# A hybrid encoder step: cached keys transposed on VectorE instead of TensorE, their loads cut in quarters on ScalarE's queue, and the sample's attention output stored once per batch

## The chip, the cores and the metric

The kernel runs on one core of one Trainium2 chip. The metric is the device time of one execution, in microseconds (us). Before the change it is 2877.0 us, the median of three runs (2876.0 to 2877.55).

## The reference

One layer of a streaming encoder is computed for two request groups that share the weights: a prompt of 2048 tokens, and a sample group of 8 batches of 16 new tokens, each batch with 1024 cached tokens. Everything is float32, D_MODEL is 1024.

```python
h = rms_norm(x, norm_g)
(a_x,a_b,a_c,a_z, g_q,g_f,g_i,g_z, s_q,s_k,s_v,s_z, m_a,m_b,m_c) = split_cols(h @ w_in)
# A: gated convolution  B: HGRN2 recurrence  C: stick-breaking attention, 8 heads of 64
z = einsum('bqhd,bkhd->bhqk', q, k) / 8
log_1mb = where(causal, log_sigmoid(-z), 0)
rest = cumsum(log_1mb, reverse) - log_1mb
A = where(causal, exp(log_sigmoid(z) + rest), 0);  o_sb = A @ v
# sample group: k = concat(cache_k (8, 1024, 8, 64), new keys), v likewise
m = sigmoid(m_a)*(o_a@wb_a) + sigmoid(m_b)*(o_b@wb_b) + sigmoid(m_c)*(o_c@wb_c)
return x + m @ w_out, and the new caches and states
```

The change touches branch C of the sample group alone: the scores of its 16 queries against the 1024 cached keys, and where its output is kept.

## The kernel before

The 17 tiles of 128 tokens (tile 0 is the sample group) are projected in three groups. In each group a list of jobs runs over the columns of `w_in`. A job multiplies a slice of weights with the normalised, transposed tokens: `proj_chan` (the matmul at L710, 24 of them for one accumulator) or `proj_tok` (L721). There are two accumulators in PSUM, which ScalarE or VectorE empty. To keep float32 accuracy every product is three passes over a high and a low part. The split weights of the first group are stored in DRAM (`W`) and loaded again by the later groups, 1 MB at a time (L208) or in two halves (L201); three weight buffers stand ready.

Other work is written as Python generators that the matmul loops advance: each `yield` returns a cost, and a background queue runs as far as its credit allows. So the place of a step in the program is set by these costs. `hbg` holds the recurrence of branch B (matmul L1039 between VectorE steps L1028 to L1040), `bg` the attention; in the second group `bg` holds `sample_attention()`, which this change is about. A planner of the tile framework then fixes the order on each engine from what it expects to be ready, so that an instruction can run ahead of others that the code has earlier. At run time every engine and every DMA queue works through its own order, and an instruction that waits holds back all behind it.

`sample_attention()` walks over 8 batches with three segments each (24 in all), of 3, 3 and 2 blocks of 128 cached tokens, so 64 blocks. For a segment:

- `keys(m)` brings the keys into the form that the scores need, head dimension on the partitions. Per block, SyncE issues one load of 256 KB (L455; 128 tokens by 512 columns, 2 KB per row) into `kc` (three buffers, shared with a few loads at either end), TensorE transposes it in four 128 by 128 pieces into PSUM (L458), and ScalarE copies the bank into `kt` (L459; two buffers of one segment each). The generator then yields a cost of 1.3.
- `scores` multiplies queries and keys (L476) and applies the two sigmoids on ScalarE (L483, L485), the scan and the product on VectorE (L489, L490).
- `turned` transposes the weights of a segment (L499) and loads the values (L506); `values` multiplies them (L522).

After the last segment of a batch the accumulator holds 128 rows (8 heads by 16 tokens) by 128 columns, of which each row needs one half of 64. ScalarE copies it to `od`, and eight stores of SyncE (L529), one per head, put the 16 by 64 pieces in their place in `OCS` (128 tokens by 512). At the end one load (L548) brings `OCS` back, and four transposes and a gate finish the branch.

## Time and profile before

| | |
|---|---|
| median of the runs | 2877.0 us |
| the profiled execution | 2876.11 us, its span 2873.2 us |
| TensorE (matmul) busy | 2853.0 us, 99% of the span |
| VectorE, ScalarE, GpSimd busy | 1546.5 us (54%), 1018.7 us (35%), 331.8 us (12%) |
| granted TensorE clock | 1.00 |
| moved by DMA | 649.76 MB in 370475 packets, mean 226 GB/s |
| first and last transpose of cached keys (L458) | 599.1 and 1138.5 us |

The page gives for each engine the time in which it had an instruction under way, and then follows the work that ended last back through what released each step. A wait counts only where it is on that chain. The DMA share is the mean busy share of the core's 16 DMA engines; it can read a little over 1, since packets overlap in an engine. A packet is one contiguous piece; 33481 of the packets are under 512 bytes, nearly all of them the reports of a DMA's end, up to 16 for each DMA.

### The profile page before, as it was taken

The page shows a single profiled execution, that of the slowest core. Times are in us where ns is not written, and L with a number is a line of the kernel's source. Part 1 is how long each engine was busy: PE and PEld are TensorE (multiplying, and loading weights), DVE is VectorE, ACT ScalarE, POOL GpSimd, SP SyncE. Part 2 cuts the span into 40 slices and gives each one's busy share as a digit, 9 for nine tenths or more (in the row PEclk, how much of TensorE's full clock was granted, in tenths as well). Part 3 has the DMA queues.
Part 4 walks back from the last instruction along what each step waited for, and adds up shares of the span by engine and source line. Part 5 has one row for each costly group of instructions (what it writes and reads, how often), then busy time and mean ns, then how long its engine had stood idle before and what let it go on. Part 6 is the DMA issues. An engine that isn't in the chain of part 4 may idle for free.

```text
span 2873.2 us, 51723 instructions
## 1 busy us (share of the span) xinstructions
PE 2853.0 (99%) x19479; PEld 2662.3 (93%) x19479; DVE 1546.5 (54%) x3304; ACT 1018.7 (35%) x2375; POOL 331.8 (12%) x802
## 2 busy tenths in 40 slices
PE   9999999999999999999999999999999999999999
PEld 9999999999999999999999999999998888787888
DVE  5454635641344442545434747557485876867743
ACT  4333222242233332213334444434444444544420
POOL 3110000111200000001323111111010011010100
PEclk9999999999999999999999999999999999999999
DMA  8887777777678887746766454544447877878876
GB/s 306 305 276 247 231 241 244 231 243 243 212 249 266 276 265 243 243 167 192 237 215 202 146 173 136 173 139 151 144 145 238 286 234 239 266 250 266 271 250 210
DMA packets 370475, 649.76 MB, mean 226 GB/s; under 512 B 33481, under 2 KB 246306, under 8 KB 339506
## 3 DMA queue, kind: packets, MB, share of 16 engines
q1 hardware_dynamic: 369458, 644.36, 68.2%
q8 instruction: 154, 2.52, 0.4%
q0 software_dynamic: 768, 2.10, 0.2%
q14 instruction: 95, 0.78, 0.1%
HBM read 447.06 MB, written 199.27 MB: 225 GB/s over the span
## 4 chain that ended last, share of the span: by engine, by line
PE 76%; DVE 2%; DMA 2%; issue 1%; ACT 0%; POOL 0%; SPq 0%; DVEq 0%; POOLq 0%; ACTq 0%
PE acc L710 33%; PE acc L721 10%; PE acc L1440 9%; PE acc L1471 6%; PE pv L359 4%; PE tp L310 4%; PE z L330 2%; PE z L329 2%; PE z L1039 1%; PE tp L458 1%; DMA gate<-GM 1%; PE pv L522 1%; PE z L476 0%; PE hg L1086 0%; PE hg L826 0%
## 5 line engine op out<-in xcount | busy, mean ns | idle before, releaser
L710 PE MATMUL acc<-hx,w 128*128 128x384 f32 (+1 forms) x6816 | 1251.8, 333 | 0.1
L710 PEld LDWEIGHTS acc<-hx,w 128*128 128x128 f32 x6816 | 1106.5, 188 | 21.9 <-issue 15.2
L721 PE MATMUL acc<-w,hx 128*128 128x256 f32 x2544 | 328.6, 284 | 1.8 <-DVE hx L176 0.9
L342 DVE TENSOR_TENSOR_SCAN pr<-snb,carry 128x513 f32<-128x513 f32 x192 | 246.5, 1284 | 153.3 <-ACT snb L333 151.7
L721 PEld LDWEIGHTS acc<-w,hx 128*128 128x128 f32 x2544 | 310.9, 188 | 5.0 <-DVE hx L176 1.7
L311 ACT COPY aT<-tp 128x512 f32<-128x512 f32 (+2 forms) x320 | 167.6, 524 | 375.2 <-PE tp L310 361.3
L710 PE MATMUL acc<-hx,wst 128*128 128x384 f32 x1248 | 247.2, 344 | 0.0
L1440 PE MATMUL acc<-o,w 128*128 128x512 f32 (+2 forms) x1080 | 234.7, 363 | 1.8 <-DMA o<-OX 1.8
L333 ACT ACTIVATE snb<-z 128x512 f32<-128x512 f32 (+2 forms) x320 | 172.4, 539 | 144.5 <-PE z L330 140.4
L710 PEld LDWEIGHTS acc<-hx,wst 128*128 128x128 f32 x1248 | 215.4, 188 | 6.4 <-issue 3.7
L1440 PEld LDWEIGHTS acc<-o,w 128*128 128x128 f32 x1080 | 185.1, 188 | 33.8 <-issue 5.3
L347 DVE TENSOR_TENSOR sp<-sp,pr 128x512 f32<-128x512 f32 (+2 forms) x320 | 195.3, 611 | 29.2 <-POOL sp L338 3.7
L342 DVE TENSOR_TENSOR_SCAN pr<-snb,one 128x129 f32<-128x129 f32 (+3 forms) x128 | 114.4, 894 | 123.9 <-POOL snb L338 123.6
L310 PE MATMUL tp<-idf,sp 128*128 128x128 f32 x1088 | 171.3, 273 | 2.5 <-ACT aT L311 1.5
L335 ACT ACTIVATE sp<-z 128x512 f32<-128x512 f32 (+2 forms) x320 | 171.5, 536 | 0.0
L1471 PE MATMUL acc<-w,mh 128*128 128x256 f32 x816 | 161.2, 285 | 1.0 <-DVE yt L1479 0.8
L1176 ACT ACTIVATE gm<-acc 128x384 f32<-128x384 f32 (+1 forms) x144 | 68.2, 474 | 230.4 <-PE acc L710 197.5
L310 PEld LDWEIGHTS tp<-idf,sp 128*128 128x128 f32 x1088 | 131.8, 141 | 19.3 <-issue 4.4
L176 DVE TENSOR_TENSOR w<-wst,w 128x1024 fp32r<-128x1024 f32 x72 | 88.1, 1223 | 110.7 <-ACT w L175 107.9
L1471 PEld LDWEIGHTS acc<-w,mh 128*128 128x128 f32 x816 | 131.0, 188 | 7.2 <-issue 4.2
L329 PE MATMUL z<-Kt,Q 128*128 128x512 f32 (+2 forms) x320 | 128.8, 403 | 0.3 <-ACT sp L335 0.2
L359 PE MATMUL pv<-aT,Vt 128*64 128x512 f32 (+3 forms) x640 | 128.1, 535 | 0.0
(299 smaller groups left out, 3570.1 us busy)
## 6 DMA issues: line engine op xcount, KB each, us to landing
w<-W SPq DMA_DIRECT2D x168, 1024.0 KB, 6.0
W<-w SPq DMA_DIRECT2D x72, 1024.0 KB, 5.0
wst<-W SPq DMA_DIRECT2D x112, 512.0 KB, 5.1
wst<-in_w_in_dram SPq DMA_DIRECT2D x72, 512.0 KB, 5.1
GM<-gm SPq DMA_DIRECT2D x120, 192.0 KB, 3.7
W<-mwp SPq DMA_DIRECT2D x40, 512.0 KB, 4.2
Kt<-KT SPq DMA_DIRECT2D x160, 128.0 KB, 3.1
o<-OX SPq DMA_DIRECT2D x72, 256.0 KB, 4.7
```

Source lines behind the costliest of these rows:

```text
L310: nc.tensor.transpose(tp[:, j * P:(j + 1) * P], sp[:, j * P:(j + 1) * P], idf)
L311: nc.scalar.copy(aT[:, e, 0:nb, i * P:(i + 1) * P], tp[:, :w].rearrange("p (b q) -> p b q", q=P))
L329: nc.tensor.matmul(z[:, :w], Q1[:, i * P:(i + 1) * P], Kt[:, :w], start=True, stop=False)
L333: nc.scalar.activation(sn[:, 512 - w:512], z[:, :w], AF.Sigmoid, scale=-0.125)
L335: nc.scalar.activation(sp[:, :w], z[:, :w], AF.Sigmoid, scale=0.125)
L342: nc.vector.tensor_tensor_scan(pr[:, 512 - w:513][:, ::-1], s_in, s_in, one if diag else carry[e][i], ALU.mult, ALU.bypass)
L347: nc.vector.tensor_tensor(sp[:, :w], sp[:, :w], pr[:, 513 - w:513], ALU.mult)
L359: nc.tensor.matmul(pv[64 * e:64 * e + 64, c0:n], Vt[:, j, e], aT[:, e, j, c0:n], start=first and j == 0, stop=last and j == nb - 1, skip_g ...
L710: nc.tensor.matmul(acc[:, :n], w[0][a][:, k], hT[b][:, k, :n], start=k == 0 and i == 0, stop=k == KB - 1 and i == 2)
L721: nc.tensor.matmul(acc[:, :256], hT[b][:, k, ti * P:(ti + 1) * P], w[k // 4][a][:, k % 4], start=k == 0 and i == 0, stop=k == KB - 1 and i ...
L1440: nc.tensor.matmul(acc[:, :n], w[0][a][:, k, dd * P:(dd + 1) * P], box[x][b][:, k, sl], start=k == 0 and i == 0, stop=k == 3 and i == 2)
L1471: nc.tensor.matmul(acc[:, :256], box["l" if b else "h"][:, k, ti * P:(ti + 1) * P], w[k // 4][a][:, k % 4], start=k == 0 and i == 0, stop= ...
```

## The change

1. `kc` becomes four-dimensional (128 partitions; 4 pairs of heads, 4 groups of 32 tokens, 32 columns), the same 256 KB. The one load on SyncE's queue becomes four loads on ScalarE's queue, one per quarter of 32 partitions. Quarter `a` fetches, for each of the 128 tokens and each pair of heads, the 32 columns of that quarter: contiguous pieces of 128 bytes.
2. The four TensorE transposes and ScalarE's copy out of PSUM become one VectorE transpose that turns every 32 by 32 block of `kc` and writes `kt`. What the 128 by 128 transpose did across blocks, the address pattern of the loads does.
3. `OCS` keeps the whole `od` of a batch (128 by 128) in one store instead of eight; at the end eight loads, one per head, pick the halves instead of one load.

The costs of the yields stay as they are.

```diff
-    OCS = dram.tile([P, 512], F32, name="OCS")
+    OCS = dram.tile([NB, P, 2, 64], F32, name="OCS")
...
             for bi in range(blocks(m)):
                 blk = 3 * sg + bi
-                kc = sa.tile([P, 512], F32, tag="cst", name="kc", bufs=3)
-                nc.sync.dma_start(kc, cache_k[0, b, blk * P:(blk + 1) * P].rearrange("t h d -> t (h d)"))
-                tp = ps_tp()
-                for h in range(4):
-                    nc.tensor.transpose(tp[:, h * P:(h + 1) * P], kc[:, h * P:(h + 1) * P], idf)
-                nc.scalar.copy(kt[:, :, bi * P:(bi + 1) * P], tp.rearrange("p (h t) -> p h t", h=4))
+                kc = sa.tile([P, 4, 4, 32], F32, tag="cst", name="kc", bufs=3)
+                keys_ = cache_k[0, b, blk * P:(blk + 1) * P].rearrange("(c p) h d -> p c (h d)", p=32)
+                keys_ = keys_.rearrange("p c (h x) -> p h c x", x=P)
+                for a in range(4):
+                    nc.scalar.dma_start(kc[32 * a:32 * a + 32], keys_[:, :, :, 32 * a:32 * a + 32])
+                nc.vector.transpose(kt[:, :, bi * P:(bi + 1) * P].rearrange("p h (c q) -> p h c q", q=32), kc)
                 yield 1.3
...
                 nc.scalar.copy(od, pv[:, 0:P])
-                for h in range(8):
-                    nc.sync.dma_start(OCS[b * TS:(b + 1) * TS, h * 64:(h + 1) * 64],
-                                      od[h * TS:(h + 1) * TS, 64 * (h % 2):64 * (h % 2) + 64])
+                nc.sync.dma_start(OCS[b].rearrange("r e d -> r (e d)"), od)
...
         oc = sa.tile([P, 512], F32, tag="cst", name="oc", bufs=3)
-        nc.sync.dma_start(oc, OCS)
+        for h in range(8):
+            nc.sync.dma_start(oc[:, h * 64:(h + 1) * 64], OCS[:, h * TS:(h + 1) * TS, h % 2])
```

## Rows read from the trace of the kernel before

**Rows 1.** The page: busy time by engine; shares of the last chain by line.

```profile
PE 2853.0 (99%) x19479; PEld 2662.3 (93%) x19479; DVE 1546.5 (54%) x3304; ACT 1018.7 (35%) x2375; POOL 331.8 (12%) x802
...
PE acc L710 33%; PE acc L721 10%; PE acc L1440 9%; PE acc L1471 6%; PE pv L359 4%; PE tp L310 4%; PE z L330 2%; PE z L329 2%; PE z L1039 1%; PE tp L458 1%; DMA gate<-GM 1%; PE pv L522 1%; PE z L476 0%; PE hg L1086 0%; PE hg L826 0%
```

**Rows 2.** Chain of waits, 560 to 1150 us: by line; one piece (start, us).

```profile
by line: PE acc L710 56.0%; PE acc L721 23.2%; PE tp L458 4.8%; PE pv L522 3.1%; PE z L476 2.4%; PE z L1039 2.1%; PE tp L499 1.3%; PE hg L826 0.9%; DMA xt<-in_x_prompt_dram 0.7%; PE hg L1086 0.5%; PE tp L1088 0.5%; PE hg L1084 0.5%; PE z L1
...
818.53 4.42 PE acc L710 x24
```

**Rows 3.** Stretches: start:end, length, busy us of each engine, granted clock, DMA share, GB/s.

```profile
560.00:1150.00 590.00, 587.23 (x4588) 566.38 (x4587) 226.15 (x587) 187.50 (x469) 52.38 (x92) 1.00 0.76 250
...
560.00:580.00 20.00, 19.39 (x130) 18.77 (x128) 10.64 (x35) 4.76 (x11) 3.96 (x4) 1.00 0.86 298
...
1060.00:1080.00 20.00, 20.00 (x147) 18.45 (x140) 2.87 (x4) 6.74 (x14) 0.00 (x0) 1.00 0.91 306
...
1120.00:1140.00 20.00, 20.00 (x147) 19.05 (x147) 8.41 (x23) 6.70 (x18) 0.00 (x0) 1.00 0.82 283
```

**Rows 4.** The timeline from 842 to 867 us: start, us, engine, line, operation.

```profile
842.78 0.42 DVE L1046 TENSOR_TENSOR Kd<-hgk,X 128x256 f32<-128x256 f32 x1
...
843.12 0.30 DVE L1040 COPY_PREDICATED sc<-lmask,z 128x128 f32<-128x128 int32 x1
...
845.03 0.47 PEld L458 LDWEIGHTS tp<-idf,kc 128*128 128x128 f32 x4
...
845.47 1.00 PEld L710 LDWEIGHTS acc<-hx,w 128*128 128x128 f32 x6
...
845.77 0.33 SPq L455 DMA_DIRECT2D kc<-in_cache_k_dram  x1
...
858.20 3.84 SPq L529 DMA_DIRECT2D OCS<-od  x8
...
866.98 0.47 PEld L458 LDWEIGHTS tp<-idf,kc 128*128 128x128 f32 x4
```

**Rows 5.** DMA packets from 560 to 1150 us: count, MB, sizes.

```profile
DMA packets 78082, 147.57 MB, mean 250 GB/s; under 512 B 8834, under 2 KB 43906, under 8 KB 72374
```

**Rows 6.** DMA from 205 to 206 us; queue: packets, MB, share of 16 engines.

```profile
DMA packets 603, 0.31 MB, mean 308 GB/s; under 512 B 1, under 2 KB 603, under 8 KB 603
...
q1 hardware_dynamic: 603, 0.31, 104.6%
```

**Rows 7.** DMA from 22.4 to 22.7 us, the same two rows.

```profile
DMA packets 213, 0.09 MB, mean 309 GB/s; under 512 B 146, under 2 KB 213, under 8 KB 213
...
q1 hardware_dynamic: 213, 0.09, 110.4%
```

**Rows 8.** DMA from 697.8 to 699 us, the same two rows.

```profile
DMA packets 96, 0.01 MB, mean 10 GB/s; under 512 B 96, under 2 KB 96, under 8 KB 96
...
q1 hardware_dynamic: 96, 0.01, 7.8%
```

**Rows 9.** DMA from 698.4 to 698.6 us, the same two rows.

```profile
DMA packets 4, 0.00 MB, mean 1 GB/s; under 512 B 4, under 2 KB 4, under 8 KB 4
...
q1 hardware_dynamic: 4, 0.00, 1.5%
```

**Rows 10.** Groups by line, whole span: count | busy us, mean ns | idle.

```profile
L459 ACT COPY kt<-tp 128x512 f32<-128x512 f32 x64 | 37.5, 588 | 58.6 <-PE tp L458 58.3
...
L347 DVE TENSOR_TENSOR sp<-sp,pr 128x512 f32<-128x512 f32 (+2 forms) x320 | 195.3, 611 | 29.2 <-POOL sp L338 3.7 <-DVE pr L342 0.5
```

**Rows 11.** Issue durations of the key loads on SyncE: ns min/median/max.

```profile
L455 SPq DMA_DIRECT2D kc<-in_cache_k_dram x64: 327/383/1494, 563.2 to 1119.0; - x64
```

**Rows 12.** Waits: who for whom, us in total, times, longest.

```profile
SPq L455 <- PE tp L458: 52.9, 24, 7.5
...
ACT w L175 <- DMA wst<-in_w_in_dram: 17.4, 10, 3.2
...
PE acc L1440 <- DMA o<-OX: 1.8, 1, 1.8
```

## The prediction

> **What bounds the kernel now.** I read the page first. TensorE is busy for 99% of the span, and the chain that ended last runs through its lines; the cached keys' transposes (L458) hold 1% of it [rows 1]. The change lives in one stage, so I then took the chain of waits, the table of stretches and the DMA view from 560 to 1150 us, which holds the keys' loads and transposes. There TensorE is busy 587.23 of 590 us at a granted clock of 1.00 (the level of 2.4 GHz), L458 holds 4.8% of the chain, VectorE is busy 226.15 us, ScalarE 187.50 us, and the 16 DMA engines have a mean share of 0.76 [rows 2, 3]. So two resources matter: TensorE, which sets the end, and DMA, which has a quarter to spare.
>
> **TensorE loses the transposes.** 4.8% of 590 us is 28.3 us. The timeline gives the same: weight loads of one block's transposes start at 845.03 and the next matmul's at 845.47, 0.44 us, times 64 blocks 28.2 us [rows 2, 4]. L458's whole busy time counts overlap with its neighbours twice, and I don't use it. Term: -28.3 us; no cover hides it, because TensorE has the next matmul at hand, but something else may take its place.
>
> **DMA gets small packets.** 64 blocks times 4 loads times 512 pieces (32 tokens, 4 groups, 4 pairs) are 131072 packets of 128 bytes. They replace 64 x 128 = 8192 packets of 2 KB. What goes: 0.76 x 16 x 590 us moved 147.57 MB, so 20.6 GB/s for an engine, 99.6 ns for 2 KB, and 8192 x 99.6 / 16 = 51 us of all engines [rows 3, 5]. What comes has no row, so I bound it. From 205 to 206 us there are only packets of 512 bytes: 1.046 x 16 x 1000 ns / 603 = 27.8 ns [rows 6]. From 22.4 to 22.7 us 146 packets are smaller (the gains' broadcast loads of 256 bytes) and 67 have 512: 1.104 x 4800 ns = 5299, less 67 x 27.8, leaves 23.5 ns each, on a full DMA [rows 7]. From 697.8 to 699 us the only traffic is the old OCS store, 256-byte pieces and as many end reports: 1498 ns / 96 = 15.6 ns on average [rows 8]; four reports alone take 1.5% of 3200 ns, 12 ns each [rows 9], which leaves 19.2 for 256 bytes on an idle DMA. 128 bytes therefore lie between 12 ns (a report) and 27.8 ns (a packet of 512). Carrying each pair half-way on gives 15.6 ns idle (between 12 and 19.2) and 21.4 ns full (as far below 23.5 as half of the step from 27.8). The stage is between the two; I take 18.5 ns, so 131072 x 18.5 / 16 = 152 us, plus 192 further loads' reports (2 us): net +103 us of all engines. At the ends: +49 us and +179 us.
>
> The stage had 0.76 x 590 = 448 us of DMA work; it would have 551 us in 590 - 28 = 562 us, 98% on average. That is not even: the 29 stretches of 20 us between 560 and 1140 lie between 0.51 and 0.91, 0.86 in the first and 0.82 in the last, mean 0.77 [rows 3]. Spreading the 103 us evenly (3.5 us to each) and setting each stretch against 19.04 us, 16 of the 29 overflow by 18.8 us together; if a full DMA reads 1.05, as it does with 512-byte packets [rows 6], 9 overflow by 6.4 us. The loads are a segment ahead, not more (the load issued at 845.77, right behind the transposes that free its buffer, is for the block transposed at 866.98 [rows 4], three blocks on), so little is smoothed between stretches. Term: +12.6 us, the middle; ends 0 (12 ns) and 49 to 74 us (27.8 ns), for which I take 62.
>
> The Trainium skill ("DMA: Bandwidth & Descriptors", Specifications) states that transfers below 512 bytes are slower, as the DMA engine reads, modifies and writes there. By that rule 128 bytes cost no less than 512 do. The trace agrees only in part: 256-byte pieces took 19.2 to 23.5 ns against 27.8. The rule's result is the second rival.
>
> **ScalarE gets issues, loses copies.** The 64 copies go, 37.5 us [rows 10]. 256 issues come. No load is issued on ScalarE before; on SyncE the issue of a key load takes 0.383 us, at least 0.327 [rows 11], and eight OCS stores in a row take 3.84 us, 0.48 each [rows 4]. So 84 to 123 us, and ScalarE goes from 187.5 to 234 to 273 us of 562: it is no bound, but its queue stands still in lumps. A block's four issues hold it for up to 1.9 us, a segment's twelve for 5.8 us if they come together, and behind them wait the copies and sigmoids that empty accumulators. An accumulator takes 4.42 us to fill [rows 2], and there are two, so one lump of four is covered, and twelve in a row delay the next by up to 5.8 + 0.5 - 4.4 = 1.9 us. Over 24 segments that is 0 to 46 us. I take 5, near the lower end, because loads wait for buffers that free one at a time as VectorE finishes.
>
> **VectorE gets 64 transposes.** There is no such row. A pass over 128x512 in float32 with two inputs takes 0.611 us [rows 10]; four predicated copies of 128x128 would be 1.2 us [rows 4]. So 39 to 77 us; I take 39, the same shape. VectorE then has 265 us of 562 and is no bound. The new wait is the transpose's, for four loads: behind it stand the recurrence's steps, for whose results TensorE waits (L1039). Whether it bites depends on the order. The planner does move instructions: L1046 starts at 842.78, before L1040 at 843.12, which the code has first [rows 4]. Where ScalarE waits for loads placed in this manner, 10 of 72 were late, 17.4 us together, at most 3.2 [rows 12]: 0.24 us for each, which for 64 blocks is 15 us at most and 0 if loads are a segment ahead. It is in the 5 us above.
>
> **SyncE and the sample's output.** SyncE loses 64 issues and stands 52.9 us less behind key buffers [rows 12], and 64 stores become 8 (8 x 0.48 us less 0.48, for each batch); at the end seven loads come, 3.4 us, after seven stores fewer. Only weight and activation loads gain, and TensorE waited for those 1.8 us in the whole run [rows 12]: 0, and at most 1.8 us won.
>
> **Sum.** -28.3 + 12.6 + 5 = -10.7 us. The profiled execution took 2876.1 us, its span 2873.2, and the median is 0.9 above it. From the median: 2866 us. Its own range runs from the full relief, 2848, to where a measurement can't tell it from no change (0.2%, 5.8 us), 2871.
>
> **Rivals.** (1) TensorE's time goes wholly to DMA and queue waits: the two plus terms come to 22 to 34 us instead of 17.6, which the 18.8 us of overflow and 5 to 10 for the queues already make. For it: an average of 98% with 16 full stretches. Against: a full DMA reads 1.05. 2877 us.
>
> (2) Small packets cost as much as 512 bytes do, by packet and not by bytes. DMA then has 627 us of work in a stage of 562 us, and keys come late in nearly every stretch: -28.3 + 62 = +34, 2911 us, up to +70 if the DMA only fills to 95%. For it: halving the packet from 512 to 256 saved only 4.3 of 27.8 ns. Against: an idle DMA took 19.2. It decides the sign from about 20 ns on if nothing is smoothed.
>
> (3) ScalarE's queue: twelve issues stand together in each segment, or wait for a key buffer, while an accumulator waits to be emptied. 24 x 1.9 = 46 us: -28.3 + 12.6 + 46 = +30, 2907 us. It turns the sign once a segment costs TensorE (28.3 - 12.6) / 24 = 0.65 us. For it: nothing on that queue was ever issued before, and the order there was free of such lumps. Against: ScalarE is idle for two thirds of the stage.
>
> That the transposes stay on TensorE's path in another form can't be: L458 is gone.
>
> **How the numbers follow.** The forecast has 0.45, rival (1) 0.19, (2) 0.19, (3) 0.17. That makes faster by over 0.2% 0.45, within 0.2% 0.19, slower 0.36. The range runs from 2848 (all relief, no cost) to 2925, past the centres of both slower rivals; above it stay their tails.
>
> **What would show it.** Right: L458 and L459 gone, the stretch from 599 to 1139 us shorter by 10 to 28 us, a DMA share there above 0.9, some 204000 packets there in place of 78082, TensorE without long idle times. Packet price: a share over 1 with idle TensorE behind keys would show rival (2). TensorE waiting for ScalarE's copies, with DMA issues ahead of them on its queue, shows rival (3). VectorE idle behind the loads of `kc`, with TensorE waiting for L1034 to L1040, would make my placing of the wait wrong. A VectorE transpose well above 1.2 us would make its term wrong.

## The result and the profile after

The changed kernel took 2886.93 us (median of 12 runs), the kernel before 2874.90 us in the 12 runs beside them: ratio 1.0040, 95% interval [1.0029, 1.0051]. It is slower by 12.0 us where I had forecast faster by 10.7 us. The range held the time, but only because it was drawn past the slower rivals; the sign was wrong. The profiled execution took 2884.56 us, its span is 2882.7 us.

The page of the changed kernel: busy time by engine and shares of the last chain by line (old L710, L721 and L1440 are now L711, L722 and L1441).

```profile
PE 2838.9 (98%) x19223; PEld 2643.8 (92%) x19223; DVE 1583.8 (55%) x3368; ACT 984.0 (34%) x2311; POOL 331.2 (11%) x802
...
PE acc L711 27%; PE acc L1441 10%; PE acc L722 8%; PE acc L1472 7%; PE pv L360 4%; PE tp L311 4%; DMA kc<-in_cache_k_dram 3%; PE z L331 2%; PE z L330 2%; PE z L1040 1%; DMA vc<-in_cache_v_dram 1%; DMA xt<-in_x_prompt_dram 1%; PE pv L524 0%;
```

Against [rows 1] the transposes' line is gone from the chain and TensorE is busy 14 us less, but the span is 9.5 us longer, and the keys' transfers (`kc`) hold 3% of the chain, which [rows 1] does not have. The next view is the table of stretches, with the columns of [rows 3].

```profile
560.00:1150.00 590.00, 563.86 (x4274) 539.46 (x4273) 260.52 (x643) 151.95 (x402) 50.30 (x88) 0.99 0.88 248
...
960.00:980.00 20.00, 20.00 (x156) 19.65 (x155) 12.36 (x41) 4.48 (x13) 0.00 (x0) 1.00 1.10 284
...
1060.00:1080.00 20.00, 19.69 (x127) 18.33 (x123) 4.18 (x6) 4.25 (x9) 0.00 (x0) 0.95 0.84 222
...
1140.00:1160.00 20.00, 17.29 (x112) 15.68 (x111) 12.21 (x39) 4.25 (x10) 0.21 (x1) 0.83 0.63 185
```

TensorE is busy 563.86 of 590 us, where before it was busy 587.23 [rows 3]; 26 us of it are idle now. The granted clock, 1.00 in every stretch before, is 0.95 and 0.83 in two that hold pauses of TensorE. Its levels are 1.2 and 2.4 GHz, so 0.83 is what a third of the stretch at the lower one gives. DMA's mean share went from 0.76 to 0.88 while the rate fell from 250 to 248 GB/s [rows 3]; five of the 31 stretches of 20 us from 560 to 1180 read 1.01 to 1.10, the last of them at 960. The packets of this stage, as in [rows 5], and the two queues that carry most:

```profile
DMA packets 202403, 146.38 MB, mean 248 GB/s; under 512 B 141232, under 2 KB 176813, under 8 KB 196717
...
q1 hardware_dynamic: 66893, 128.08, 67.7%
q10 hardware_dynamic: 135168, 16.79, 19.5%
```

The new queue, q10, is ScalarE's. Its 135168 packets are the 131072 pieces of 128 bytes and 4096 reports, in 19.5% of 16 x 590 us: 13.6 ns for a packet.

The chain of waits from 560 to 1180 us, by line, beside [rows 2]; below it, who waited for whom in this stretch (us in total, times, longest).

```profile
by line: PE acc L711 32.3%; PE acc L722 15.8%; DMA kc<-in_cache_k_dram 15.4%; DMA vc<-in_cache_v_dram 2.9%; PE pv L524 2.3%; DMA mwx<-in_w_out_dram 2.3%; PE z L478 2.0%; DMA xt<-in_x_prompt_dram 1.9%; issue 1.7%; DMA mwx<-in_w_branch_dram 1
```

```profile
DVE kt L461 <- DMA kc<-in_cache_k_dram: 112.7, 30, 9.5
...
ACT gm L1177 <- DMA kc<-in_cache_k_dram: 23.9, 5, 6.7
...
ACT mwp L176 <- DMA mwx<-in_w_branch_dram: 16.6, 8, 6.3
...
ACT mwp L176 <- DMA mwx<-in_w_out_dram: 11.4, 4, 4.2
...
PE z L478 <- DVE kt L461: 6.5, 2, 4.5
```

The keys' loads, of which [rows 2] has none, hold 15.4% of the chain. VectorE stood idle 112.7 us in front of 30 of its 64 transposes until keys landed. ScalarE's gate copies (`gm`, L1177) read no keys, yet they came late behind `kc`, because the key loads' issues stand ahead of them in ScalarE's queue. And the merge weights' fetch (`mwx`), issued on SyncE, came late for ScalarE by 28 us, where before it was 5.9 us:

```profile
ACT mwp L175 <- DMA mwx<-in_w_out_dram: 3.9, 2, 2.3
...
ACT mwp L175 <- DMA mwx<-in_w_branch_dram: 2.0, 2, 1.7
```

The issues on ScalarE and the transposes on VectorE (ns, min/median/max, first and last start):

```profile
L460 ACTq DMA_DIRECT2D kc<-in_cache_k_dram x256: 585/587/2599, 560.1 to 1140.3; - x128
...
L461 DVE STREAM_TRANSPOSE kt<-kc x64: 669/711/715, 570.9 to 1149.7; 128x512 f32<-128x512 f32 x64
```

One block from near to, first on ScalarE's timeline (start, us, engine, line, operation, in brackets the idle time before it and its releaser), then on all engines. The four quarters of this block are the load at 1045.14 and the three from 1047.85 on.

```profile
1045.14 0.59 ACTq L460 DMA_DIRECT2D kc<-in_cache_k_dram  x1
...
1047.85 2.58 ACTq L460 DMA_DIRECT2D kc<-in_cache_k_dram  x3
...
1054.32 3.28 ACTq L460 DMA_DIRECT2D kc<-in_cache_k_dram  x2
```

```profile
1058.14 0.71 DVE L461 STREAM_TRANSPOSE kt<-kc 128x512 f32<-128x512 f32 x1 [8.59 <-DMA kc<-in_cache_k_dram]
...
1058.90 1.51 PE L478 MATMUL z<-kt,qz 128*32 128x384 f32 x8 [4.45 <-DVE kt L461]
```

The last quarter's issue ends at 1050.4, the transpose begins at 1058.14 after 8.59 us of idle VectorE, and TensorE's scores (L478) begin behind it after 4.45 us of idle TensorE. That is the wait that took the transposes' place.

To see where the time goes I matched the n-th accumulator matmul of the stage's lines in both traces. At 559 us of the kernel before the changed one is 1.4 us early, at 615 us 1.5 late, at 969 us 6.8 early, at 1086 us 3.2 late and at 1184 us 11.0 late; after that it stays between 10.5 and 11.0 us until 2800 us. The whole loss is made among the keys. Three numbers account for it: the relief, 25 us (experiment e2_rows_sp); the time from 555 to 1300 us in which neither a matmul nor a weight load was under way, less the 2.8 us of before; and the sum of 20 us x (1 - granted clock) over the stretches of 20 us from 540 to 1300 us. Here -25 + 25.3 + 10.6 = 10.9 us, against 11.0 measured. Of the kernels below, those with the relief (9.4 us of it where 24 blocks have the change) close to 3 us in the same way, but for e1_sp_quarters, which is 17 us later than this sum; the three without it that lose time miss it by 5 to 7 us.

### The profile page after: what moved, and what is told of

Same layout as the page of the kernel before. It is cut to its first block, busy times and chain, and to the rows that moved or that the text cites. A ratio compares the mean times of both kernels' runs of the same rounds, so it can differ in the third digit from the quotient of the medians.

```text
span 2882.7 us, 51381 instructions
## 1 busy us (share of the span) xinstructions
PE 2838.9 (98%) x19223; PEld 2643.8 (92%) x19223; DVE 1583.8 (55%) x3368; ACT 984.0 (34%) x2311; POOL 331.2 (11%) x802
## 3 DMA queue, kind: packets, MB, share of 16 engines
q10 hardware_dynamic: 135168, 16.79, 4.0%
## 4 chain that ended last, share of the span: by engine, by line
PE 69%; DMA 7%; DVE 3%; issue 1%; ACT 1%; POOL 0%; ACTq 0%; SPq 0%; DVEq 0%; POOLq 0%
PE acc L711 27%; PE acc L1441 10%; PE acc L722 8%; PE acc L1472 7%; PE pv L360 4%; PE tp L311 4%; DMA kc<-in_cache_k_dram 3%; PE z L331 2%; PE z L330 2%; PE z L1040 1%; DMA vc<-in_cache_v_dram 1%; DMA xt<-in_x_prompt_dram 1%; PE pv L524 0%; DMA mwx<-in_w_out_dram 0%; DVE pr L343 0%
## 5 line engine op out<-in xcount | busy, mean ns | idle before, releaser
L711 PE MATMUL acc<-hx,w 128*128 128x384 f32 (+1 forms) x6816 | 1252.0, 333 | 0.7 <-ACT gm L1177 0.3
L711 PEld LDWEIGHTS acc<-hx,w 128*128 128x128 f32 x6816 | 1113.6, 189 | 25.3 <-issue 16.7
L722 PE MATMUL acc<-w,hx 128*128 128x256 f32 x2544 | 328.2, 284 | 3.2 <-DVE gm L1137 1.6
L722 PEld LDWEIGHTS acc<-w,hx 128*128 128x128 f32 x2544 | 311.2, 188 | 6.3 <-DVE gm L1137 1.8
L711 PE MATMUL acc<-hx,wst 128*128 128x384 f32 x1248 | 247.8, 345 | 0.9 <-DVE hgz L1137 0.9
L1441 PE MATMUL acc<-o,w 128*128 128x512 f32 (+2 forms) x1080 | 234.7, 363 | 1.4 <-issue 1.4
L711 PEld LDWEIGHTS acc<-hx,wst 128*128 128x128 f32 x1248 | 217.2, 189 | 7.8 <-issue 3.7
L1441 PEld LDWEIGHTS acc<-o,w 128*128 128x128 f32 x1080 | 185.0, 188 | 33.4 <-issue 4.8
L1177 ACT ACTIVATE gm<-acc 128x384 f32<-128x384 f32 (+1 forms) x144 | 68.4, 475 | 232.0 <-PE acc L711 174.0
```

Of the source, the lines that this page charges most:

```text
L711: nc.tensor.matmul(acc[:, :n], w[0][a][:, k], hT[b][:, k, :n], start=k == 0 and i == 0, stop=k == KB - 1 and i == 2)
L722: nc.tensor.matmul(acc[:, :256], hT[b][:, k, ti * P:(ti + 1) * P], w[k // 4][a][:, k % 4], start=k == 0 and i == 0, stop=k == KB - 1 and i ...
L1441: nc.tensor.matmul(acc[:, :n], w[0][a][:, k, dd * P:(dd + 1) * P], box[x][b][:, k, sl], start=k == 0 and i == 0, stop=k == 3 and i == 2)
```

## The experiments

Each was timed in five rounds beside the kernel before. "Late" is the distance of the accumulator matmuls from before once the stage is over, "idle" and "clock" are the two numbers just described, "ahead" is the median time from the end of a block's last issue to its transpose, and "in front" is the median time from a buffer's release (the transpose three blocks back) to the first issue into it.

| run | ratio to before, 95% | late | idle | clock | in front | ahead |
|---|---|---|---|---|---|---|
| before | 1 | 0 | 2.8 | 0 | 0.5 | 21.3 |
| the change | 1.0040 [1.0029, 1.0051] | 11.0 | 28.1 | 10.6 | 12.8 | 6.0 |
| e4_ocs_only | 1.0007 [0.9998, 1.0015] | 1.0 | 3.9 | 0 | | |
| e2_rows_sp | 0.9920 [0.9906, 0.9933] | -25.0 | 3.1 | 0 | 1.4 | 18.9 |
| e5_rows_act | 0.9945 [0.9931, 0.9959] | -14.7 | 9.1 | 3.4 | 0.0 | 21.3 |
| e6_four_2kb | 0.9977 [0.9968, 0.9986] | -6.9 | 15.4 | 5.2 | 2.2 | 16.8 |
| e7_one_128 | 1.0035 [1.0023, 1.0047] | 14.3 | 28.6 | 14.0 | 0.0 | 22.2 |
| e3_quarters_pe | 1.0284 [1.0267, 1.0301] | 74.2 | 52.6 | 17.4 | | |
| e1_sp_quarters | 1.0341 [1.0327, 1.0355] | 97.5 | 69.7 | 38.4 | 17.8 | 7.3 |
| e8_ahead | 1.0107 [1.0093, 1.0120] | 36.4 | 43.8 | 19.0 | 11.0 | 6.4 |
| e9_pool | 1.0000 [0.9990, 1.0009] | -0.1 | 19.7 | 10.6 | 1.6 | 14.2 |
| e10_third | 0.9997 [0.9988, 1.0006] | 0.8 | 9.4 | 3.4 | | |
| e12_pool_lead | 0.9972 [0.9961, 0.9983] | -6.1 | 16.1 | 7.0 | 1.6 | 13.1 |
| e11_third_pool | 0.9974 [0.9963, 0.9984] | -7.3 | 3.6 | 1.8 | | |
| e13_lead_only | 1.0001 [0.9992, 1.0010] | -0.8 | 2.5 | 0 | 0.5 | 21.3 |
| e15_act_lead | 1.0071 [1.0056, 1.0085] | 18.7 | 30.3 | 15.6 | 13.0 | 6.0 |
| e14_third_lead | 0.9975 [0.9967, 0.9984] | -6.1 | 4.4 | 1.8 | | |
| e16_spare | 1.0092 [1.0075, 1.0109] | 25.0 | 18.2 | 3.4 | | |
| e17_spare_pool | 1.0123 [1.0106, 1.0140] | 34.4 | 28.1 | 14.0 | | |

In e2, e5 and e6 (loads of whole rows), in e3 (quarters, turned by TensorE) and in e7 (one load of pieces) the keys reach `kt` in another order than the scores need; bytes, shapes and instructions are as told, and their time alone counts.

### The parts one by one

**e1_sp_quarters**: the change with the quarter loads back on SyncE.

```diff
-                    nc.scalar.dma_start(kc[32 * a:32 * a + 32], keys_[:, :, :, 32 * a:32 * a + 32])
+                    nc.sync.dma_start(kc[32 * a:32 * a + 32], keys_[:, :, :, 32 * a:32 * a + 32])
```

> The changed kernel with the four quarter loads of a block issued on SyncE's queue instead of ScalarE's. Three theories of the lost time. Theory A (issue and order): the four issues of a block are spread over 6.4 us of ScalarE's queue, the transpose stands at the head of VectorE's order and waits for the last of them (112.7 us in 30 waits), and TensorE waits behind VectorE. Theory B (crowding): 131072 small packets slow all other transfers. Theory C (ScalarE held): 256 issues of 0.59 us keep ScalarE from emptying accumulators. A: the issues stand closer together, the waits of VectorE for keys fall below 60 us, ratio to the kernel before 0.994 to 1.000. B: no change, 1.003 to 1.006. C: ScalarE is free again, 0.993 to 0.998, with the waits of VectorE for keys as before.

Measured: 1.0341, the slowest of all and far above what any of the three theories gave. In the chain of 560 to 1180 us the key loads' own issues on SyncE have 4.9% and the weights' loads behind them 4.5%.

```profile
by line: PE acc L711 40.7%; PE acc L722 19.2%; SPq L460 4.9%; DMA w<-W 4.5%; PE pv L524 2.9%; issue 2.4%; PE z L478 2.3%; PE z L1040 1.8%; POOL rr L235 1.7%; DVE pr L491 1.2%; PE tp L501 1.0%; PE hg L827 1.0%; DMA vc<-in_cache_v_dram 0.9%; 
```

So it is not ScalarE's queue as such that spoils the change: the same loads on SyncE's queue, in which weights, values and stores go out in order, leave the kernel 97.5 us late in place of 11.0. Their place in SyncE's order differs too: a block's first issue stands 20 other DMAs later than the one load of e2_rows_sp does (median of the 64 blocks).

**e2_rows_sp**: VectorE's transposes alone; the keys come in one load of 2-KB rows on SyncE, as before.

```diff
-                for a in range(4):
-                    nc.scalar.dma_start(kc[32 * a:32 * a + 32], keys_[:, :, :, 32 * a:32 * a + 32])
+                nc.sync.dma_start(kc.rearrange("p h c q -> p (h c q)"),
+                                   cache_k[0, b, blk * P:(blk + 1) * P].rearrange("t h d -> t (h d)"))
```

> The changed kernel with one load per block again, rows of 2 KB on SyncE's queue; VectorE's transposes stay. The keys then stand in the wrong order, so the scores against cached keys are not the reference's; their time is what counts. It bounds what the transposes' leaving TensorE is worth: all three theories say 0.990 to 0.994 (17 to 28 us less than before). If VectorE's waits for keys stay near 110 us and the ratio is over 0.997, the place of the transpose in VectorE's order is to blame, whatever the loads are like.

Measured: 0.9920, 25.0 us early. The stretch of 620 us, and the wait of VectorE for keys:

```profile
560.00:1180.00 620.00, 616.81 (x4698) 595.23 (x4697) 295.23 (x758) 166.81 (x448) 55.27 (x99) 1.00 0.78 259
```

```profile
DVE kt L461 <- DMA kc<-in_cache_k_dram: 1.2, 2, 1.0
```

TensorE is busy 616.81 of 620 us at a clock of 1.00, and VectorE waits 1.2 us in all for keys. The relief is real, VectorE's 64 transposes cost nothing, and what the change loses it loses by its loads.

**e3_quarters_pe**: the other half alone; quarter loads on ScalarE, transposes on TensorE and copies on ScalarE as before.

```diff
-                nc.vector.transpose(kt[:, :, bi * P:(bi + 1) * P].rearrange("p h (c q) -> p h c q", q=32), kc)
+                tp = ps_tp()
+                for h in range(4):
+                    nc.tensor.transpose(tp[:, h * P:(h + 1) * P], kc[:, h].rearrange("p c q -> p (c q)"), idf)
+                nc.scalar.copy(kt[:, :, bi * P:(bi + 1) * P], tp.rearrange("p (h t) -> p h t", h=4))
```

> The changed kernel with its quarter loads on ScalarE's queue, but transposed on TensorE and copied by ScalarE as before the change. The keys come out in the wrong order, so the scores against cached keys are not the reference's. It takes the loads' cost alone. Theory A: TensorE's transposes stand late in its order and don't feel late loads, so little is lost: 1.000 to 1.004. Theory B: the loads cost as much as in the changed kernel and the relief is gone: 1.010 to 1.015. Theory C: the same, 1.010 to 1.018, with TensorE waiting for accumulators.

Measured: 1.0284, 74.2 us late, above every theory. TensorE itself now waits for keys, 26.4 us in 16 waits of its transposes; the loads are 20.9% of the chain.

```profile
by line: PE acc L714 33.0%; DMA kc<-in_cache_k_dram 20.9%; PE acc L725 18.1%; PE tp L463 4.7%; PE pv L527 2.4%; PE z L481 2.3%; issue 2.3%; DMA KT<-kt 1.9%; DMA w<-W 1.9%; DMA xt<-in_x_prompt_dram 1.5%; DMA mwx<-in_w_branch_dram 1.3%; DMA Q
```

```profile
PE tp L463 <- DMA kc<-in_cache_k_dram: 26.4, 16, 4.4
```

The same loads cost 74 us where TensorE itself waits for them, and 36 (11.0 + 25) where VectorE does and TensorE only behind it: the two parts don't add.

**e4_ocs_only**: the sample's output alone (one store, eight loads), with the keys as before.

```diff
-                for h in range(8):
-                    nc.sync.dma_start(OCS[b * TS:(b + 1) * TS, h * 64:(h + 1) * 64],
-                                      od[h * TS:(h + 1) * TS, 64 * (h % 2):64 * (h % 2) + 64])
+                nc.sync.dma_start(OCS[b].rearrange("r e d -> r (e d)"), od)
...
-        nc.sync.dma_start(oc, OCS)
+        for h in range(8):
+            nc.sync.dma_start(oc[:, h * 64:(h + 1) * 64], OCS[:, h * TS:(h + 1) * TS, h % 2])
```

> The kernel before with the third part of the change alone: one store of the sample's output per batch and eight loads at the end. All theories say no change, 0.998 to 1.001; the forecast put it at 0 to 1.8 us won.

Measured: 1.0007 [0.9998, 1.0015]: no difference that shows.

### How many loads, and how small their pieces

**e5_rows_act**: one load of 2-KB rows, but on ScalarE (the edit of e2_rows_sp with `nc.scalar`).

> The changed kernel with one load per block, rows of 2 KB, issued on ScalarE's queue; VectorE's transposes stay. The keys stand in the wrong order, so the scores against cached keys are not the reference's. Against the one on SyncE's queue it shows what ScalarE's queue does to one load, against the changed kernel what quarters and small packets do. Theory A: one issue instead of four spread ones, 0.992 to 0.998. Theory B: as on SyncE's queue, 0.990 to 0.994. Theory C: a quarter of the issues, 0.993 to 0.997.

Measured: 0.9945, 10 us behind the same load on SyncE and in the ranges of theories A and C. ScalarE stops in front of these issues for their buffers: 40.2 us in 38 stops, summed over its timeline from 560 us on, of which 35 (36.6 us) end when the transpose three blocks back does.

**e6_four_2kb**: four loads on ScalarE, each of 32 whole rows.

```diff
-                    nc.scalar.dma_start(kc[32 * a:32 * a + 32], keys_[:, :, :, 32 * a:32 * a + 32])
+                    t0 = blk * P + 32 * a
+                    nc.scalar.dma_start(kc[32 * a:32 * a + 32].rearrange("p h c q -> p (h c q)"),
+                                        cache_k[0, b, t0:t0 + 32].rearrange("t h d -> t (h d)"))
```

> The changed kernel with four loads of 32 partitions per block on ScalarE's queue as it has them, but each of whole rows of 2 KB: four issues, few large packets. The keys stand in the wrong order, so the scores against cached keys are not the reference's. With one load of such rows on the same queue the ratio was 0.9945, with the quarters in 128-byte pieces 1.004. Theory A (four issues spread over ScalarE's order make the last quarter late): 1.001 to 1.005, VectorE waiting for keys as in the changed kernel. Theory B (the small packets make it): 0.993 to 0.997, VectorE waiting under 20 us for keys.

Measured: 0.9977, 8 us behind one load and between the ranges of the two theories; VectorE waits 9.5 us for keys, as theory B had it. An issue takes 0.320 us; ScalarE stops 105.6 us in 83 stops in front of them, nearly all for earlier DMAs and not for buffers (see e8_ahead); yet the keys are 16.8 us ahead of their use.

```profile
L461 ACTq DMA_DIRECT2D kc<-in_cache_k_dram x256: 317/320/1789, 560.5 to 1086.3; - x128
```

**e7_one_128**: one load of 2048 pieces of 128 bytes on ScalarE (with rows of 33 columns in `kc`, so that the pieces stay apart).

```diff
-                kc = sa.tile([P, 4, 4, 32], F32, tag="cst", name="kc", bufs=3)
+                kc = sa.tile([P, 16, 33], F32, tag="cst", name="kc", bufs=3)
...
+                rows_ = cache_k[0, b, blk * P:(blk + 1) * P].rearrange("t h d -> t (h d)")
+                nc.scalar.dma_start(kc[:, :, 0:32], rows_.rearrange("t (g q) -> t g q", q=32))
...
```

> The other half: one load of 128 partitions per block on ScalarE's queue, cut into 128-byte pieces (2048 packets) by a padded destination of 33 columns per piece: one issue, small packets, the same bytes. The keys stand in the wrong order, so the scores against cached keys are not the reference's. Theory A: one issue, little spread, 0.994 to 0.998. Theory B: 1.001 to 1.006, with the share of the small packets' queue near 19% and VectorE waiting around 100 us for keys. If both this and the four loads of 2 KB rows come out near 0.995, it takes the two together.

Measured: 1.0035, as slow as the change, but in another way. One issue holds ScalarE for 1.544 us at the median and 6.103 us at most, and the issues, not the transfers, are in the chain (4.3% against 2.7%).

```profile
L460 ACTq DMA_DIRECT2D kc<-in_cache_k_dram x64: 547/1544/6103, 560.4 to 1094.0; - x64
```

```profile
by line: PE acc L712 41.0%; PE acc L723 21.0%; ACTq L460 4.3%; DMA mwx<-in_w_branch_dram 2.9%; PE pv L525 2.7%; DMA kc<-in_cache_k_dram 2.7%; PE z L479 2.2%; DVE kt L461 1.6%; issue 1.6%; PE z L1041 1.5%; PE tp L502 1.2%; DMA KT<-kt 1.0%; D
```

The keys are 22.2 us ahead, and VectorE waits 11.1 us for them in all, where theory B, whose range holds the time, had about 100. So four loads of rows keep their lead (16.8 us), one load of pieces keeps it too (22.2 us), and only four loads of pieces lose it (6.0 us). This alone doesn't show that it takes both, since the order of ScalarE's instructions differs too (next experiment).

**e8_ahead**: the change with each block's loads put three blocks ahead in the program, behind the transpose that frees their buffer.

```diff
...
+                while len(coming) < 3 and todo:
+                    fetch()
+                kc = coming.pop(0)
                 nc.vector.transpose(kt[:, :, bi * P:(bi + 1) * P].rearrange("p h (c q) -> p h c q", q=32), kc)
+                fetch()
```

> The whole change, results as the reference's, with the quarter loads issued three blocks ahead in the program: the first three blocks before the first transpose, then each block's loads right behind the transpose that frees its buffer. If the keys are late only because their loads are issued late (theory A in its wide form: it is the lead and not the amount of DMA), VectorE's waits for keys fall below 40 us and the ratio to 0.992 to 0.999. If the small packets themselves slow the other transfers (theory B), it stays at 1.001 to 1.006.

Measured: 1.0107, worse by 25 us and above both theories. The lead did not come: a buffer still waits 11.0 us for its first issue, and the keys are 6.4 us ahead. ScalarE's own work comes later still behind them:

```profile
DVE kt L472 <- DMA kc<-in_cache_k_dram: 103.0, 26, 9.2
...
ACT gm L1189 <- DMA kc<-in_cache_k_dram: 36.2, 6, 13.8
```

The edit moved the loads in the program, but hardly in ScalarE's own order, which the planner fixes. Counted in ScalarE's other instructions, a block's first issue stands 3 earlier than in the change (median of the 64 blocks; 19 stand where they stood). In e5_rows_act, e6_four_2kb and e7_one_128 it stands 15.5 to 16.5 earlier. So this run doesn't test an earlier issue, and the three others have, besides larger or fewer loads, an earlier place for them. Why the planner gave the change's loads a later place isn't on record, and no run holds the order fixed.

What the issues wait for stands in the trace: each DMA names the semaphore, a counter, on which its end is counted, and those that it waits for. SyncE's and ScalarE's DMAs together use eight semaphores in turn, 268 or 269 DMAs on each in the change. 230 of the 256 key loads wait for their own semaphore, that is for the DMA that had it before, whichever queue that was on; so do 1897 of 2002 DMAs on SyncE before the change. For VectorE, that is for a free buffer, 18 first quarters wait and one second quarter. In front of the change's key loads ScalarE stood 73.7 us in 57 stops (summed from 560 to 1150 us, those over 0.15 us). Of these, 54 with 73.2 us ended within 0.1 us of the landing of the earlier DMA on the load's own semaphore: 46.6 us behind an earlier key load, 26.6 us behind a DMA of SyncE. In e8_ahead it is 87.0 of 90.2 us, 49.5 us of them behind SyncE; in e6_four_2kb 98.8 of 105.6 us. DMAs that GpSimd issues have eight semaphores of their own.

### Another queue, and fewer blocks

**e9_pool**: the change with the quarter loads on GpSimd (`nc.gpsimd.dma_start`, nothing else).

> The whole change with the quarter loads issued on GpSimd's queue, results as the reference's. By now: rows of 2 KB on SyncE's queue give 0.992, so the transposes' relief is there; the quarters lose it, on ScalarE's queue (1.004) and far more on SyncE's (1.034). Theory D (queues): the small packets harm what stands behind their issue on the same queue, ScalarE's copies there, the weights' loads here; on GpSimd's queue, with little work behind them, the ratio falls to 0.992 to 0.998. Theory B (crowding of the DMA engines by 131072 packets, whoever issues them): 1.000 to 1.006. If GpSimd is slow to issue them, its own busy time and VectorE's waits for keys show it, and the ratio goes over 1.006.

Measured: 1.0000 [0.9990, 1.0009], 11 us better than on ScalarE, above the range of theory D and at the lower end of theory B's. A buffer waits 1.6 us for its first issue in place of 12.8, the keys are 14.2 us ahead, and VectorE waits 4.5 us for them. What is left is the other late transfer:

```profile
by line: PE acc L711 39.8%; PE acc L722 18.1%; DMA mwx<-in_w_branch_dram 12.2%; PE pv L524 2.5%; PE z L478 2.1%; DMA OCS<-od 2.0%; PE z L1040 1.8%; issue 1.4%; DMA QT<-kt 1.4%; DMA KT<-kt 1.1%; DMA xt<-in_x_prompt_dram 1.0%; ACT mwp L176 1.
```

```profile
ACT mwp L176 <- DMA mwx<-in_w_branch_dram: 32.8, 11, 8.1
...
DVE kt L461 <- DMA kc<-in_cache_k_dram: 4.5, 4, 2.9
```

The merge weights hold 12.2% of the chain. These loads also take less of the DMA engines than ScalarE's. The queue's 8480 packets are 4096 of 4 KB for the keys, as many reports of 4 bytes and 288 packets of other loads; they take 13.2% of 620 us. So two things change with the queue, what stands around the issues and the form of the packets, and this run doesn't separate them.

```profile
q0 software_dynamic: 8480, 17.58, 13.2%
```

**e10_third**: the change for the first block of each segment only, 24 of 64, on ScalarE; the other 40 by the code of before.

```diff
+                if bi == 0:
+                    ... (the change, as it is)
+                else:
+                    ... (the lines of before)
```

> The change for the first block of each segment alone (24 of 64 blocks, quarter loads on ScalarE's queue), the other blocks as before the change on SyncE's queue, TensorE and ScalarE; results as the reference's. The relief of TensorE is 24 x 0.44 = 10.6 us. If the loss grows faster than the number of such blocks, since the loads then have time to land between them (9.2 us for a block, 10.0 us from first issue to last packet in the changed kernel), most of the relief is kept: 0.996 to 0.999. If each block costs the same wherever it stands, 24/64 of the change's loss: 1.001 to 1.002.

Measured: 0.9997, between the two ranges. The relief, 24/64 of 25 = 9.4 us, went again into idle time (6.6 us) and clock (3.4 us).

**e12_pool_lead**: e9_pool, with the merge weights fetched one step further ahead, into two buffers.

```diff
...
+            x = mw.tile([P, 512], F32, tag="mwx", name="mwx", bufs=2)
...
+            if j + 1 < len(halves):
+                fetch(halves[j + 1][0])
             yield
+            x = coming.pop(0)
```

To make room for the second buffer the edit also puts the attention's causal mask into one of the three buffers that the keys use (`cst`).

> The key loads on GpSimd as in the run at 1.0000, and the merge weights' fetch (mwx) put one step of split_merge_weights further ahead, in two buffers. Theory: what is left against the gain is transfers that come late beside 128-byte pieces, and there the merge weights: ScalarE waited 32.8 us in 11 waits for mwx, and DMA mwx stood with 12.1% in the chain of the stage. With the lead those waits fall below 8 us, TensorE's idle time in 555 to 1300 us from 19.7 to about 8 us, the granted clock loses about 5 us in place of 10, and the time is 0.994 to 0.996 of before. Rival, that the lost time comes of GpSimd itself (it issues 229 us in this stage, and its own tables and gathers come later): the wait of ScalarE goes, TensorE waits for something else, and the time stays at 0.999 to 1.001.

Measured: 0.9972 [0.9961, 0.9983], 2867.02 us: faster than both kernels, though less than expected: between the theory's range and the rival's. ScalarE's wait for the weights went from 32.8 to 0.3 us, and idle time only from 19.7 to 16.1 us.

```profile
ACT mwp L176 <- DMA mwx<-in_w_branch_dram: 0.3, 1, 0.3
```

```profile
by line: PE acc L712 48.9%; PE acc L723 17.8%; DMA W<-mwp 4.5%; PE pv L525 2.9%; PE z L479 2.1%; DMA KT<-kt 2.1%; DMA xt<-in_x_prompt_dram 1.9%; PE z L1041 1.8%; issue 1.7%; DMA QT<-kt 1.5%; PE tp L502 1.1%; POOL rr L235 0.9%; SPq L550 0.8%
```

In their place the store of the split weights (`W<-mwp`, 4.5%) ends late. The weights aren't late by the small pieces alone: in e6_four_2kb, whose loads have none, ScalarE waits 28.0 us for them too.

**e11_third_pool**: e10_third with the loads on GpSimd.

> The new keys for the first block of each segment only (24 of 64 blocks), its loads issued on GpSimd; the other 40 blocks as before. Theory (lateness grows with how densely the small pieces come, and 24 blocks leave them 25 us each): TensorE's relief is 24/64 of 25 = 9.4 us, idle time and clock lose 3 to 5 us, time 0.997 to 0.998. Rival (the loss goes with the number of blocks, as the gain): three eighths of the GpSimd run's difference, 1.000 plus or minus 0.001, as the same third on ScalarE's queue gave 0.9997.

Measured: 0.9974 [0.9963, 0.9984], 2866.90 us: the other version that beats both. Nearly the whole relief is kept; the clock is 1.00 and idle time 3.6 us.

```profile
560.00:1180.00 620.00, 616.33 (x4743) 594.27 (x4742) 266.83 (x687) 184.50 (x475) 124.06 (x193) 1.00 0.79 252
```

**e13_lead_only**, **e15_act_lead**, **e14_third_lead**: the earlier fetch of the merge weights (the edit of e12_pool_lead) in the kernel before, in the change as it is, and in e11_third_pool.

> The kernel before with nothing but the earlier fetch of the merge weights (mwx, two buffers). Theory (the fetch is late only beside 128-byte pieces): before, ScalarE waited for mwx some 6 us in this stage and TensorE was idle 2.8 us in 555 to 1300 us, so there is nothing to win: 0.999 to 1.001. Rival (the earlier fetch is a gain by itself, and the run at 0.9972 owes it to that): 0.997.

> The whole change, quarter loads on ScalarE as it has them, with the earlier fetch of the merge weights. Theory (ScalarE is held by 166 us of issues and VectorE waits for keys; the weights are the smaller part): the waits of ScalarE for mwx, 28 us, go, but TensorE's idle time stays above 20 us and the time at 1.001 to 1.004. Rival (late weights are the larger part): as on GpSimd the time falls by 0.003 or more, to 1.001 or less, with the idle time below 20 us.

> The first block of each segment by the change on GpSimd, the other 40 as before, with the earlier fetch. Theory (24 blocks already leave TensorE idle only 3.6 us and the clock 1.8 us, so the lead has nothing to mend): 0.997 to 0.998 as without it. Rival (the two gains add): 0.995.

Measured: 1.0001, 1.0071 and 0.9975. The fetch is worth nothing without the change, so the 8 us of e12_pool_lead over e9_pool are won back from it; and it does not mend the change on ScalarE, where VectorE still waits 90.4 us for keys. There it even costs 8 us, which neither theory had; where these go isn't shown (ScalarE's stops in front of key loads, 68.0 us, are even shorter than in the change).

```profile
DVE kt L462 <- DMA kc<-in_cache_k_dram: 90.4, 27, 9.9
...
ACT gm L1178 <- DMA kc<-in_cache_k_dram: 11.9, 2, 6.6
...
ACT mwp L176 <- DMA mwx<-in_w_branch_dram: 1.1, 1, 1.1
```

**e16_spare**, **e17_spare_pool**: the kernel before with three more loads of 4 KB per key block, to a tile that nothing reads, on ScalarE and on GpSimd.

```diff
+                for a in range(3):
+                    spare = sa.tile([P, 32], F32, tag="spare", name="spare", bufs=12)
+                    nc.scalar.dma_start(spare[0:32], cache_k[0, b, blk * P + 32 * a:blk * P + 32 * a + 32, 0, 0:32])
```

> The kernel before, unchanged, with 192 further loads of 4 KB (three per key block, 32 pieces of 128 bytes, to a tile that nothing reads) issued on ScalarE. They add 6144 small packets, under 1% of what the stage moves. Theory (a share of the loss is that each further DMA takes one of eight semaphores from the DMAs of both queues, so that ScalarE stands in front of its issues and SyncE's loads go out later): ScalarE stands 30 us or more in front of these issues, TensorE is idle 8 to 20 us in 555 to 1300 us in place of 2.8, and the time is 1.002 to 1.006. Rival (only the number of small pieces matters): 0.999 to 1.001, idle time within 2 us of before.

> The same 192 further loads issued on GpSimd, whose DMAs use eight semaphores of their own. Theory of the shared semaphores: 0.999 to 1.001. Rival (further DMAs cost by what they add to the 16 DMA engines, on whichever queue they are issued): the same ratio as with ScalarE, within 0.001.

Measured: 1.0092 and 1.0123. The first half of the theory held, and by more than expected: 192 loads that move next to nothing cost 25 us, and ScalarE stood 32.6 us in front of them, in 26 stops from 560 us on, each until the earlier DMA on the load's semaphore landed. The second half fell: on GpSimd, without semaphores shared with SyncE, they cost 34 us, which the rival's "same ratio" didn't have either; there 186 of the 192 wait for the GpSimd DMA that had their semaphore before. The chain names both, the transfers and, on GpSimd, the issues:

```profile
by line: PE acc L713 49.4%; PE acc L724 15.2%; DMA spare<-in_cache_k_dram 9.9%; PE tp L461 4.2%; PE pv L525 2.7%; PE z L479 2.0%; ACTq L458 1.9%; PE z L1042 1.7%; PE tp L502 1.1%; DMA wst<-W 0.9%; DMA KT<-kt 0.8%; issue 0.8%; PE tp L1091 0.
```

```profile
by line: PE acc L713 48.7%; PE acc L724 18.6%; DMA spare<-in_cache_k_dram 7.1%; POOL spare L458 6.9%; PE tp L461 4.1%; PE pv L525 2.7%; PE z L479 1.9%; PE z L1042 1.7%; issue 1.3%; POOL rr L234 1.3%; PE tp L502 1.2%; PE hg L829 0.9%; DMA w<
```

As nothing tied them to the keys they went out in a crowd (172 of the 192 on ScalarE between 560 and 707 us), each engine's own work behind them. That an issue holds up the work behind it is shown for both engines. What the shared semaphores cost by themselves these two runs don't tell; the pair e5_rows_act and e6_four_2kb gives 8 us for three more loads per block, their issues and their stops together.

## Why the prediction was wrong

**TensorE's relief, -28.3 us: right.** Alone it gives 25.0 us (e2_rows_sp); the chain's share had priced it 13% too high.

**VectorE's transposes: right.** 0.711 us at the median against 0.61 taken, and no cost of its own. **The sample's output at nothing: right** (e4_ocs_only).

**The packet's price, 18.5 ns: too high.** It took 13.6 ns, 111 us of all engines for the pieces in place of 152, net +63 in place of +103. My count of overflowing stretches would then have given 0.4 to 3.5 us in place of 12.6. The Trainium skill ("DMA: Bandwidth & Descriptors", Specifications), by which a transfer under 512 bytes is read, modified and written back, had made rival (2): I had concluded from it that a piece costs no less than a packet of 512 bytes. The trace has half of that, 13.6 ns against 27.8 [rows 6]; per byte, though, it is 2.2 times the price of a 2-KB packet (13.6 / 128 against 99.6 / 2048).

**The failed step: the loads as "a segment ahead", and with it the 5 us for queue and wait.** I took the lead from the old load, issued at 845.77 for a transpose at 866.98 [rows 4], and carried it over to four loads on another queue. The lead is not a property of the program's loop; it was a result of SyncE getting to the issue 0.5 us after the buffer came free. On ScalarE the first of four issues comes 12.8 us after, the four are spread over 6.4 us, and the last is 6.0 us ahead of its use where the one load was 21.3. The first issue itself doesn't stop (0 at the median): its buffer has been free for 10.6 us (median) when the last issue of the block before it ends. From first issue to last packet a block takes 10.0 us, and a block is due every 9.2 us. Full DMA engines don't explain it: the mean share was 0.88, and the 18 us lost between 969 and 1184 us fall, but for the rest of the stretch at 960, in stretches of 0.51 to 0.95. I had asked whether the bytes fit in a stretch and not whether a transfer lands in time.

I had placed the wait rightly (VectorE idle behind `kc`, TensorE behind its scores) and priced it at 0.24 us a block, from ScalarE's waits for `wst` [rows 12], at most 15 us. Together with the ScalarE stops and the late merge weights it cost 25.3 us of TensorE, against 17.6 us for both plus terms. The other 10.6 us are the granted clock, below 1 where TensorE pauses, for which I had no term at all. Sum: -25 + 25.3 + 10.6 = +11, where I had -10.7.

**The rivals.** (1), all eaten, is nearest in size. (2)'s price fell, its sign and its place (keys late) came true. (3) is half of it: ScalarE's issues do take 0.587 us each instead of 0.383 to 0.48, 166 us in all, and gate copies come late behind them, but in stops for earlier DMAs (73.2 of 73.7 us) rather than in lumps of twelve; on SyncE it would have been far worse (e1_sp_quarters).

What is shown: the loss is in the loads (e2_rows_sp against the change), it comes as late keys, late gate copies and late merge weights, and ScalarE's stops in front of the key loads are waits for earlier DMAs on their semaphores. On GpSimd, where the packets differ too, the same loads cost 11 us less (e9_pool), and the earlier fetch of the merge weights wins 6 to 8 us there (e12, e13). What stays open: how much of the late keys the small pieces, the number of issues with their stops, and the later place in ScalarE's order make each, since e5 to e7 change the order along with the loads; and why e8_ahead and e15_act_lead are slower than the change.

The Trainium skill ("Trainium Kernel Development and Optimization", Key Constraints) says that loads issued on several engines' queues share the 16 DMA engines and that spreading them saves only the issue time. Here the same 256 loads cost 1.0341, 1.0040 and 1.0000 on three queues, and the best of them has the longest issues (0.827 us against 0.587). So the time of the issues doesn't order the three; besides, what stands around an issue in its queue differs and, on GpSimd, the form of the packets, and no run here separates these.

## What to carry to other kernels

Before moving a load to another queue or cutting it up, read from the trace how long its buffer stood free before the issue and how long the data lay ready before its use; that lead, not the engines' mean share, is what the new loads must keep. Small pieces were cheaper for the DMA engines than I took them and dearer for everything that waits in line behind their issues, so apply such a change to as many blocks as the slack carries: 24 of 64 on GpSimd's nearly idle queue won 7 to 9 us, all 64 there won nothing, and all 64 on ScalarE's lost 12. And when an edit moves or splits a load, compare where its issue stands in its engine's order before comparing times: here the planner moved it too.

## What the runs showed of the hardware

- A piece of 128 bytes took 13.6 ns of a DMA engine, a 2-KB packet 99.6 ns; issued by GpSimd the same loads appear as 4096 packets of 4 KB, 32 pieces in each; with the queue's few other packets they took 13.2% of the engines' time in 620 us, where ScalarE's took 19.5% in 590 us.
- The issue of a load on ScalarE took 0.32 us for 32 rows of 2 KB, 0.587 us for 512 pieces and 1.54 us for 2048 pieces, up to 6.1 us; GpSimd took 0.827 us for 512.
- A DMA that waited for the earlier DMA on its semaphore was issued 0.02 to 0.1 us after that one landed (54 stops of ScalarE in the change).
- VectorE turned 128x512 float32 in 32 by 32 blocks in 0.70 to 0.71 us at the median.
- 192 loads of 4 KB, under 1 MB in all, cost 25 us on ScalarE and 34 us on GpSimd when they went out in a crowd.
